# Layer-two norm: squares taken per column half, roots by a third-order step and Newton, other distances at the layer boundary, lambda moved

## The chip, the cores and the metric

One core of one Trainium2 chip runs the whole program. The metric is the device time of one execution in microseconds. The kernel before has three timed runs, 758.97, 760.33 and 760.14, median 760.14; one further execution was taken by the profiler, and its trace is read below. PE is TensorE (matrix products), DVE VectorE, ACT ScalarE, POOL GpSimd, SP the queue that issues transfers.

## The reference

The program is a trunk of two layers over 512 tokens of width 1024, in float32, then a final norm. Cut to what matters here:

```python
def rms_norm(x, g):
    return x * lax.rsqrt(jnp.mean(x * x, axis=-1, keepdims=True) + EPS) * g

# layer 1 (Mamba-2): y is the scan's output, z the gate, 8 groups of 256 columns
u = y * silu(z)
u = u * lax.rsqrt(mean of u*u over each group + EPS) * gate_norm_g
x = x + u @ w_out

# layer 2 (differential attention), 8 heads of width 128, two maps per head
k, v = split(rms_norm(x, kv_norm_g) @ w_kv)
q, gate = split(rms_norm(x, b_norm_g) @ w_in)
lam = exp(sum(lf[0] * lf[1])) - exp(sum(lf[2] * lf[3])) + lambda_init
weights = softmax(scores_1) - lam * softmax(scores_2)
out = rms_norm(weights @ v, sub_g) * (1 - lambda_init)       # per head
x = x + (out * silu(gate)) @ w_out
return rms_norm(x, final_norm_g)
```

Both norms at the head of layer 2 have the same root, so x is normed once, and the two gains go into the weights.

## The kernel before

Tokens are four tiles of 128 (`t`), columns of x two halves of 512 (`n`). Every product is done as three passes, on a high and a low part of each operand (`mm3`: names ending in hi/h and lo/l). A weight arrives by one 1 MB transfer on SP (`raw`), and is split piece by piece: ScalarE writes the high part (`whi`), VectorE the low part (`wlo`), 4 pieces of 512 columns or 8 of 256 (`load`, `lay`).

**Layer 1** runs over items z, g and o and eight groups (`ssd`). At a group's end the scan's parts (`pyd`, `po1`, `po2`) are summed into dx on VectorE and GpSimd, multiplied by the gate, squared on ScalarE into `ss`, the root of four chunks is taken (`rsqrt`), ScalarE applies it (`tmp <- dx, y_y`), and TensorE transposes the result (`pyt`), which ScalarE and VectorE split into yh and yl. A planner that plays through a timeline with costs of its own decides the order of the instructions on each engine here: program order is free as long as `T.on`, `V.on` and `A.on` are False.

**The layer boundary**, called the turn here. Half 0 of the last out-projection is planned with layer 1; half 1 (`last_rows`) runs in an order written by hand: `T.on`, `V.on` and `A.on` are set, so the three engines keep program order. For each tile there are twelve 512-wide products into `po3_1_t`, and then vector work is put off by a distance: `later(n, fn)` emits `fn` when n further units of TensorE work have been emitted (a 512-wide triple counts 2, a 256-wide one 1). Per tile: add (distance 1), square of all 1024 columns (4), root (9), application to the row (root + 5). The same counter paces the weight pieces: `use_b` hands out a segment's weights and queues the next segment's pieces, of which `paced` lays one after every 32/8 = 4 units. Then `turn_rows` transposes the normed row (`btp`), split into b_hi (ScalarE) and b_lo (VectorE); `v_proj(0)` needs of tile t only these rows (`pv`), and `feat_proj("k0k1")` (`pk`) needs all four.

**Layer 2** keeps TensorE in program order; VectorE and ScalarE are planned again. Each head's values are normed by `norm_head` (statistics, `rsqrt`, multiplication of `on`), transposed (`pot`), multiplied by the gate (`og`), split (oh, ol) and projected (`pb`). In the last head three tiles are normed first, and the last tile by itself (`norm_head(7, 3, 4)`). `end(i)` closes the eight half rows: add, square, product with the final gain on GpSimd (`ot`, line 887), and for each tile the last root (`rsqrt1`, names f_) and its application, on ScalarE but for one half on VectorE. `ot` goes out by SP.

Two routines take roots, both from a bit-shift guess and three Newton steps: `rsqrt` for n columns (11 VectorE instructions), and `rsqrt1` for one column (8 instructions, on a value scaled by 2 to the 26).

The program's line 52 is the helper through which instructions are recorded, so rows of the profile are told apart by their tiles; in the changed program the helper is line 53.

Of the kernel before, what the change touches and what calls it, by code (L numbers as in the profile page):

```python
# [60 lines left out]
def trunk(ctx, tc, x, x_t, par, w_dt, w_in, w_out, w_kvqg, w_bo, d_skip, lam_qk, fin_g, out):  # L61
# [58 lines left out]
    def load(i):  # L120

        seg = segs[i]
        src, gains = source(seg)
        nk = 8 if seg[0] in "vkqt" else 4
        w = 2048 // nk
        raw = wp.tile([P, nk, w], F32, tag="raw", name=f"raw{i}", bufs=2)
        fetched[0] += 1

        def split():
            hi = wp.tile([P, nk, w], F32R, tag="whi", name=f"whi{i}", bufs=2)  # L130
            lo = wp.tile([P, nk, w], F32R, tag="wlo", name=f"wlo{i}", bufs=2)
# [15 lines left out]
            return [(head, rest, k, 32 // nk) for k in range(nk)]  # L147

        if i == 0:
            for k in range(nk):  # L150
                load_x(k)
                nc.sync.dma_start(raw[:, k, :], src[:, k * w:(k + 1) * w])
        else:
            nc.sync.dma_start(raw.rearrange("p k n -> p (k n)"), src)
        return split

    def lay(piece):
        head, rest, k, _ = piece
        head(k)
        rest(k)  # L160
# [55 lines left out]
    def rsqrt(v, n, tag, bufs=2):  # L216

        y = small.tile([P, n], F32, tag=f"{tag}_y", name=f"{tag}_y", bufs=bufs)
        c = small.tile([P, n], F32, tag=f"{tag}_c", name=f"{tag}_c", bufs=bufs)
        iy = small.tile([P, n], I32, tag=f"{tag}_i", name=f"{tag}_i", bufs=bufs)  # L220
        V.tensor_scalar(out=iy, in0=v.bitcast(I32), scalar1=1, scalar2=None, op0=ALU.logical_shift_right)
        V.tensor_scalar(out=y.bitcast(I32), in0=iy, scalar1=-1.0, scalar2=float(0x5F3759DF), op0=ALU.mult, op1=ALU.add)
# [4 lines left out]
        return y  # L227

    def rsqrt1(v26, tag, bufs=2):

# [4 lines left out]
        V.tensor_scalar(out=y.bitcast(I32), in0=iy, scalar1=-1.0, scalar2=float(0x5F3759DF - 2 ** 31), op0=ALU.mult, op1=ALU.add)
        for a in (3.0, 12.0, 768.0):
            V.scalar_tensor_tensor(out=c, in0=y, scalar=v26, in1=y, op0=ALU.mult, op1=ALU.mult)
            V.scalar_tensor_tensor(out=y, in0=c, scalar=-a, in1=y, op0=ALU.add, op1=ALU.mult)
        return y
# [249 lines left out]

    decs = {}  # L490
# [21 lines left out]
    def ssd(g):  # L512
# [91 lines left out]
    lq = sm.tile([P, 4, 64], F32, name="lq")  # L604
    nc.sync.dma_start(lq.rearrange("p a d -> p (a d)"), lam_qk.rearrange("a d -> (a d)").partition_broadcast(P))
# [5 lines left out]
    lqv = lq.rearrange("p (a b) d -> p a b d", b=2)  # L611
    lp = lqv[:, :, 0]
    V.tensor_tensor(out=lp, in0=lqv[:, :, 0], in1=lqv[:, :, 1], op=ALU.mult)
    ls = sm.tile([P, 2], F32, name="ls")
    V.reduce_sum(ls, lp, axis=AX.X)
    A.activation(ls, ls, AF.Exp)
    nlam = small.tile([P, 1], F32, name="nlam", bufs=1)
    V.scalar_tensor_tensor(out=nlam, in0=ls[:, 1:2], scalar=-LAM0, in1=ls[:, 0:1], op0=ALU.add, op1=ALU.subtract)

# [39 lines left out]
    T.on = V.on = A.on = True  # L659
    dense[0] = paced(last_rows())  # L660
# [14 lines left out]
    def v_proj(n):  # L675
        wh, wl = use_b(("v", n, 0))
# [113 lines left out]
    def norm_head(h, a=0, b=NT):  # L790
# [88 lines left out]
    def end(i):  # L879
# [12 lines left out]
        V.tensor_scalar(out=v, in0=v, scalar1=2.0 ** 26 / D, scalar2=EPS * 2.0 ** 26, op0=ALU.mult, op1=ALU.add)  # L892
        r = rsqrt1(v, "f")
# [94 lines left out]
```

## Time and profile before

| | us |
|---|---|
| median of three runs | 760.14 (758.97 to 760.33) |
| the profiled execution's own time | 758.57 |
| its span, first to last instruction | 756.8 |
| TensorE busy | 729.8 (96%) |
| VectorE / ScalarE / GpSimd busy | 563.1 / 436.4 / 133.9 |
| TensorE idle, 440 to 468 us of the span (the turn) | 6.2 |
| TensorE idle, 728 to 757 us (the tail) | 14.8 |
| mean granted clock of TensorE | 0.986 |

A row of the timeline reads: start, length, engine, line, operation, output <- inputs, partitions x elements, count, and in brackets the idle time ahead of it with what released it. A row of the waits reads: who waited, for what, total us, times, longest. A row of the time windows: the window, its length, busy time and instructions (x) of PE, PE's weight loads, DVE, ACT and POOL, the granted TensorE clock (1.00 is full), the DMA share and GB/s. Starts of matmuls are exact to the next one's; their lengths overlap.

### The profile page before, as it was taken

How to read it: one execution, taken by the hardware profiler on the slowest of the kernel's cores; microseconds unless marked ns; L12 is line 12 of the kernel's file. 1: busy time of each engine (PE TensorE's matmuls, PEld its weight loads, DVE VectorE, ACT ScalarE, POOL GpSimd, SP SyncE). 2: the span in 40 equal slices, each digit the busy share in tenths (PEclk: the TensorE clock that was granted, in tenths of full speed). 3: DMA queues.
4: the chain of work that ended last, by engine and by line, in shares of the span. 5: the costliest groups of instructions: out<-in, count | busy, mean ns of one | idle time of the engine just before them, and what ended most of it. 6: DMA issues, size and time to landing. Idle time of an engine off the chain costs nothing.

```text
span 756.8 us, 10380 instructions
## 1 busy us (share of the span) xinstructions
PE 729.8 (96%) x3741; PEld 612.2 (81%) x3741; DVE 563.1 (74%) x1286; ACT 436.4 (58%) x943; POOL 133.9 (18%) x162
## 2 busy tenths in 40 slices
PE   9999989999999999999999988999999999999993
PEld 7787867888888888887878867888988888898872
DVE  5589974789769769579977557557767867885987
ACT  6848664564746427548433337567767766656534
POOL 0009251602515024150211110000000000000013
PEclk9999999999999999999999998999999999999997
DMA  9543312132313331213132201331221221132002
GB/s 324 197 159 123 112 61 108 59 116 105 112 55 119 129 136 64 108 61 111 57 112 64 77 27 57 111 112 57 79 90 56 67 101 57 56 112 82 3 0 111
DMA packets 12915, 70.84 MB, mean 94 GB/s; under 512 B 1600, under 2 KB 2112, under 8 KB 5312
## 3 DMA queue, kind: packets, MB, share of 16 engines
q1 hardware_dynamic: 12576, 70.06, 25.7%
q8 instruction: 29, 0.48, 0.3%
q14 instruction: 22, 0.18, 0.1%
q10 hardware_dynamic: 288, 0.12, 0.1%
HBM read 68.02 MB, written 2.16 MB: 93 GB/s over the span
## 4 chain that ended last, share of the span: by engine, by line
PE 75%; DVE 9%; ACT 6%; issue 6%; DMA 2%; POOL 2%; SPq 0%; ACTq 0%; POOLq 0%
PE pg L52 15%; PE po L52 14%; PE pt L52 7%; PE pz L52 6%; PE pq L52 6%; PE pk L52 6%; PE pv L52 6%; PE pb L52 5%; PE pyd L52 3%; PE sc L52 3%; DVE wlo L52 2%; DVE xc L52 2%; ACT whi L52 2%; DVE x_tok L52 1%; PE pyt L52 1%
## 5 line engine op out<-in xcount | busy, mean ns | idle before, releaser
L52 DVE SCALAR_TENSOR_TENSOR wlo<-raw,prm,whi 128x512 fp32r<-128x512 f32 (+1 forms) x256 | 153.4, 643 | 58.6 <-ACT whi L52 58.2
L52 ACT ACTIVATE whi<-raw,prm 128x512 fp32r<-128x512 f32 (+1 forms) x256 | 137.2, 605 | 61.9 <-issue 23.0
L52 PE MATMUL pg<-a_hi,whi 128*128 128x512 f32 x256 | 103.9, 406 | 0.0
L52 PE MATMUL pg<-a_lo,whi 128*128 128x512 f32 x256 | 102.5, 400 | 0.0
L52 PE MATMUL pg<-a_hi,wlo 128*128 128x512 f32 x256 | 102.2, 400 | 0.0
L52 DVE SCALAR_TENSOR_TENSOR xc<-u,prm,xc 128x511 f32<-128x511 f32 (+2 forms) x96 | 80.5, 854 | 7.1 <-ACT xc L52 6.5
L52 PEld LDWEIGHTS pg<-a_hi,whi 128*128 128x128 f32 x256 | 48.2, 188 | 11.0 <-issue 0.2
L52 PEld LDWEIGHTS pg<-a_lo,whi 128*128 128x128 f32 x256 | 48.2, 188 | 10.9 <-issue 0.2
L52 PEld LDWEIGHTS pg<-a_hi,wlo 128*128 128x128 f32 x256 | 48.1, 188 | 10.9
L887 POOL TENSOR_TENSOR ot<-x_tok,fg 128x512 f32<-128x512 f32 x8 | 10.1, 1280 | 262.8 <-DVE o__y L52 259.3
L52 PE MATMUL po<-whi,yh 128*128 128x512 f32 x128 | 51.7, 404 | 0.6 <-ACT yh L52 0.6
L52 PE MATMUL pz<-whi,a_lo 128*128 128x512 f32 x128 | 51.3, 401 | 0.0
L52 PE MATMUL po<-wlo,yh 128*128 128x512 f32 x128 | 50.9, 398 | 0.0
L52 PE MATMUL pz<-wlo,a_hi 128*128 128x512 f32 x128 | 50.8, 397 | 0.0
L52 PE MATMUL po<-whi,yl 128*128 128x512 f32 x128 | 50.6, 399 | 0.0
L52 PE MATMUL pz<-whi,a_hi 128*128 128x512 f32 x128 | 49.9, 401 | 0.0
L52 ACT ACTIVATE xc<-u,prm 128x512 f32<-128x512 f32 x32 | 25.7, 810 | 40.4 <-DVE u L52 40.4
L540 POOL TENSOR_TENSOR xe<-xdt,tok 128x256 f32<-128x256 f32 x24 | 17.7, 765 | 150.2 <-DVE xdt L52 150.2
L52 DVE CUSTOM_DVE_ANT_0 s<-sc,bias 128x128 f32<-128x128 f32 (+3 forms) x64 | 29.8, 487 | 18.1 <-PE sc L52 17.6
L52 ACT ACT_TABLE_LOAD x27 | 34.6, 1283 | 13.6 <-DVE y_c L52 5.2
L502 POOL TENSOR_TENSOR dec<-dec,tok 128x512 f32<-128x512 f32 x32 | 40.2, 1287 | 0.6
L52 PE MATMUL pv<-whi,b_hi 128*128 128x256 f32 x128 | 37.3, 291 | 0.0
(215 smaller groups left out, 1775.1 us busy)
## 6 DMA issues: line engine op xcount, KB each, us to landing
raw<-in_w_in SPq DMA_DIRECT2D x23, 1024.0 KB, 4.8
raw<-in_w_kvqg SPq DMA_DIRECT2D x16, 1024.0 KB, 4.8
dec<-acs_d SPq DMA_DIRECT2D x8, 1024.0 KB, 4.6
raw<-in_w_out SPq DMA_DIRECT2D x8, 1024.0 KB, 4.7
raw<-in_w_bo SPq DMA_DIRECT2D x4, 1024.0 KB, 4.8
xt<-in_x_t SPq DMA_DIRECT2D x8, 256.0 KB, 6.0
x_tok<-in_x SPq DMA_DIRECT2D x4, 512.0 KB, 8.7
out<-ot SPq DMA_DIRECT2D x8, 256.0 KB, 2.1
```

Of the source, the lines that this page charges most:

```text
L52: i = op(*args, **kw)
L502: GP.tensor_tensor(out=dec[:, h], in0=dec[:, h], in1=acs_tok[:, :, R * g + h].unsqueeze(2).to_broadcast([P, NQ, P]), op=ALU.subtract)
L540: GP.tensor_tensor(out=xe[:, c], in0=xdt[:, c], in1=toe_tok[:, c, hs].unsqueeze(2).to_broadcast([P, R, HD]), op=ALU.mult)
L887: GP.tensor_tensor(out=ot[t][:, hs], in0=y, in1=fg[:, hs], op=ALU.mult)
```

## The change

Four edits.

- Squares of the second norm: half 0 of each tile is squared on ScalarE right behind its add in `out_proj(3)`, with sums in `bss[:, 0]`; at the turn only half 1 (128x512) is squared, into `bss[:, 1]`. One VectorE instruction scales `bss[:, 0]` for all four tiles, and each root's first instruction adds the two.
- Roots: one routine; a third-order step and a Newton step take the place of three Newton steps: from 11 to 9 instructions for n columns, from 8 to 7 for one, which the last tile of a head now also uses. The statistics of `norm_head` take two instructions in place of three.
- Distances at the turn: square 4 to 3, root 9 to 6, application root + 5 to root + 4. The pieces of v0's weights are laid every 2 units instead of 4, those of k0k1 after 18 units and then every 2.
- Lambda's load, sums, exponential and `nlam` are emitted behind the turn, not ahead of layer 1's end.

```diff
-    def use_b(seg):
+    def use_b(seg, first=None, pace=None):
...
-            pieces.extend(loaded.pop(i + 1)())
+            new = loaded.pop(i + 1)()
+            pace = pace or 32 // len(new)
+            pieces.extend(p + (pace if k else first or pace,) for k, p in enumerate(new))
...
     def rsqrt(v, n, tag, bufs=2):
...
+        def vyy():
+            if n == 1:
+                V.scalar_tensor_tensor(out=c, in0=y, scalar=v, in1=y, op0=ALU.mult, op1=ALU.mult)
+            else:
+                V.tensor_tensor(out=c, in0=y, in1=v, op=ALU.mult)
+                V.tensor_tensor(out=c, in0=c, in1=y, op=ALU.mult)
...
-        for _ in range(3):
-            V.scalar_tensor_tensor(out=c, in0=y, scalar=-0.5, in1=y, op0=ALU.mult, op1=ALU.mult)
-            V.tensor_tensor(out=c, in0=c, in1=v, op=ALU.mult)
-            V.scalar_tensor_tensor(out=y, in0=c, scalar=1.5, in1=y, op0=ALU.add, op1=ALU.mult)
+        vyy()
+        V.scalar_tensor_tensor(out=c, in0=c, scalar=-10.0 / 3.0, in1=c, op0=ALU.add, op1=ALU.mult)
+        V.scalar_tensor_tensor(out=y, in0=c, scalar=5.0, in1=y, op0=ALU.add, op1=ALU.mult)
+        vyy()
+        V.scalar_tensor_tensor(out=y, in0=c, scalar=-64.0 / 3.0, in1=y, op0=ALU.add, op1=ALU.mult)
         return y
...
                 V.tensor_tensor(out=x_tok[:, t, ns], in0=po, in1=x_tok[:, t, ns], op=ALU.add)
+                if j == 3:
+                    sq = small.tile([P, S], F32, tag="wide", name=f"sq3_{t}", bufs=2)
+                    A.activation(sq, x_tok[:, t, ns], AF.Square, accum_out=bss[:, 0, t:t + 1])
...
-            squares(ss, t, xn[t])
+            A.activation(xn[t][:, 512:D], y, AF.Square, accum_out=bss[:, 1, t:t + 1])
...
-            V.tensor_scalar(out=v, in0=ss[:, t:t + 1], scalar1=2.0 ** 26 / D, scalar2=EPS * 2.0 ** 26, op0=ALU.mult, op1=ALU.add)
-            r = rsqrt1(v, "f")
-            later(5, lambda: A.activation(xn[t], x_tok[:, t], AF.Copy, scale=r))
-
-        later(4, square)
-        later(9, root)
+            V.scalar_tensor_tensor(out=v, in0=bss[:, 1, t:t + 1], scalar=ROOT2 / D, in1=bss[:, 0, t:t + 1], op0=ALU.mult, op1=ALU.add)
+            r = rsqrt(v, 1, "f")
+            later(4, lambda: A.activation(xn[t], x_tok[:, t], AF.Copy, scale=r))
+
+        later(1, lambda: V.tensor_tensor(out=y, in0=po, in1=y, op=ALU.add))
+        later(3, square)
+        later(6, root)
...
-        w = use_b(("o", 3, 1))
+        w = use_b(("o", 3, 1), pace=2)
...
     T.on = V.on = A.on = True
+    later(9, lambda: V.tensor_scalar(out=bss[:, 0], in0=bss[:, 0], scalar1=ROOT2 / D, scalar2=ROOT2 * EPS, op0=ALU.mult, op1=ALU.add))
...
-        wh, wl = use_b(("v", n, 0))
+        wh, wl = use_b(("v", n, 0), *((18, 2) if n == 0 else ()))
...
-        V.scalar_tensor_tensor(out=v, in0=sums[:, 0, a:b], scalar=EPS * P, in1=sums[:, 0, a:b], op0=ALU.mult, op1=ALU.mult)
-        V.tensor_tensor(out=v, in0=v, in1=ss[:, a:b], op=ALU.add)
-        V.tensor_scalar(out=v, in0=v, scalar1=1.0 / P, scalar2=None, op0=ALU.mult)
+        V.scalar_tensor_tensor(out=v, in0=sums[:, 0, a:b], scalar=ROOT2 * EPS, in1=sums[:, 0, a:b], op0=ALU.mult, op1=ALU.mult)
+        V.scalar_tensor_tensor(out=v, in0=ss[:, a:b], scalar=ROOT2 / P, in1=v, op0=ALU.mult, op1=ALU.add)
...
+    lq = cp2.tile([P, 4, 64], F32, tag="gt", name="lq", bufs=3)
+    nc.sync.dma_start(lq.rearrange("p a d -> p (a d)"), lam_qk.rearrange("a d -> (a d)").partition_broadcast(P))
...
+    A.activation(ls, ls, AF.Exp)
+    nlam = small.tile([P, 1], F32, name="nlam", bufs=1)
+    V.scalar_tensor_tensor(out=nlam, in0=ls[:, 1:2], scalar=-LAM0, in1=ls[:, 0:1], op0=ALU.add, op1=ALU.subtract)
     V.on = A.on = False
```

How the order moves, at the turn (two engines), in layer 1 and in the tail.

**The turn, VectorE** (`po_1_t` is tile t's half 1, `wlo` v0's low pieces, `b_v` the root's first instruction). Before, then changed:

```order
L52 TENSOR_TENSOR x_tok<-po_0_3_3699,x_tok 128x512
L52 SCALAR_TENSOR_TENSOR wlo_3725<-raw_3655,prm,whi_3724 128x256 x2
L52 TENSOR_TENSOR x_tok<-po_1_0_3726,x_tok 128x512
L52 SCALAR_TENSOR_TENSOR wlo_3725<-raw_3655,prm,whi_3724 128x256 x2
L52 TENSOR_SCALAR b_v_3767<-bss 128x1
```

```order
L53 TENSOR_TENSOR x_tok<-po_0_3_3686,x_tok 128x512
L53 SCALAR_TENSOR_TENSOR wlo_3707<-raw_3636,prm,whi_3706 128x256 x4
L53 TENSOR_SCALAR bss<-bss 128x4
L53 TENSOR_TENSOR x_tok<-po_1_0_3708,x_tok 128x512
L53 SCALAR_TENSOR_TENSOR wlo_3707<-raw_3636,prm,whi_3706 128x256 x2
L53 SCALAR_TENSOR_TENSOR b_v_3747<-bss 128x1
```

Four low pieces instead of two stand ahead of tile 0's add.

**The turn, ScalarE** (`xn<-x_tok,f_y` is the application, `bss<-x_tok` a square; the first `xn` number is tile 0, the second tile 1). Before, then changed:

```order
L52 ACTIVATE whi_3724<-raw_3655,prm 128x256 x2
L52 ACTIVATE xn_3751,bss<-x_tok 128x1024
L52 ACTIVATE whi_3724<-raw_3655,prm 128x256 x2
L52 ACTIVATE xn_3784,bss<-x_tok 128x1024
L52 ACTIVATE whi_3724<-raw_3655,prm 128x256
L52 ACTIVATE xn_3751<-x_tok,f_y 128x1024
```

```order
L53 ACTIVATE sq_0_3652,bss<-x_tok 128x512
L53 ACTIVATE sq_1_3668,bss<-x_tok 128x512
L53 ACTIVATE sq_2_3684,bss<-x_tok 128x512
L53 ACTIVATE sq_3_3700,bss<-x_tok 128x512
L53 ACTIVATE whi_3706<-raw_3636,prm 128x256 x5
L53 ACTIVATE xn_3740,bss<-x_tok 128x512
L53 ACTIVATE whi_3706<-raw_3636,prm 128x256 x3
L53 ACTIVATE xn_3740<-x_tok,f_y 128x1024
L53 ACTIVATE xn_3775,bss<-x_tok 128x512
```

Tile 1's square stood ahead of tile 0's application, and now stands behind it; half 0's squares are new ahead of all.

**Group 0's root chain in layer 1, ScalarE** (`dx` is the gated output, `tmp,ss<-dx` its square, `tmp<-dx,y_y` the application, `dec` the decays). Before, then changed:

```order
L52 ACT_TABLE_LOAD
L52 ACTIVATE xc_915<-xc_915 128x512
L52 ACTIVATE tmp_711,ss_710<-dx_676 128x256 x2
L52 ACT_TABLE_LOAD
L52 ACTIVATE dec_1010<-dec_1010 128x1024
L52 ACTIVATE whi_929<-raw_927,prm 128x512 x4
L52 ACTIVATE dec_1010<-dec_1010 128x1024
L52 ACT_TABLE_LOAD
L52 ACTIVATE zs_0_1179<-pz_0_923,ar_col 128x512
L52 ACTIVATE tmp_711<-dx_676,y_y 128x256 x4
```

```order
L53 ACTIVATE tmp_708,ss_707<-dx_673 128x256 x3
L53 ACTIVATE dec_1005<-dec_1005 128x1024 x2
L53 ACT_TABLE_LOAD
L53 ACTIVATE xc_910<-xc_910 128x512
L53 ACTIVATE whi_924<-raw_922,prm 128x512 x4
L53 ACTIVATE tmp_708<-dx_673,y_y 128x256 x4
```

Between the last squares and the application stood two table loads and a zs; now one table load and an xc stand there.

**The tail, VectorE** (`o__` are the last head's single root, `on` the normed values, `pb_t_n` the half rows). Before, then changed:

```order
L52 TENSOR_TENSOR x_tok<-pb_0_0_6747,x_tok 128x512
L52 SCALAR_TENSOR_TENSOR o__y<-o__c,o__y 128x1
L52 TENSOR_TENSOR x_tok<-pb_0_1_6751,x_tok 128x512
L52 SCALAR_TENSOR_TENSOR o__c<-o__y 128x1
L52 TENSOR_TENSOR o__c<-o__c,o_v_3_6766 128x1
L52 SCALAR_TENSOR_TENSOR o__y<-o__c,o__y 128x1
L52 TENSOR_TENSOR x_tok<-pb_1_0_6755,x_tok 128x512
L52 TENSOR_TENSOR on_6422<-on_6422,o__y 128x128
```

```order
L53 SCALAR_TENSOR_TENSOR o__c<-o__y,o_v_3_6729 128x1
L53 SCALAR_TENSOR_TENSOR o__y<-o__c,o__y 128x1
L53 TENSOR_TENSOR x_tok<-pb_0_0_6710,x_tok 128x512
L53 TENSOR_TENSOR on_6391<-on_6391,o__y 128x128
L53 TENSOR_TENSOR x_tok<-pb_0_1_6714,x_tok 128x512
L53 TENSOR_TENSOR x_tok<-pb_1_0_6718,x_tok 128x512
```

`on` moves from behind the third add to behind the first. TensorE's own order is unchanged from out-projection 3 to the end.

More of the change, by code (lines that the diff above doesn't have):

```diff
@@ L31 @@
 BIG = 1e30
+ROOT2 = (1024.0 / 27.0) ** 2
 ORDER_B = "v0 k0k1 q0t0 q1t1 k2k3 q2t2 v1 q3t3 k4k5 q4t4 v2 q5t5 k6k7 q6t6 b0 v3 q7t7 b1 b2 b3".split()
@@ L145, in rest @@
                     V.tensor_tensor(out=lo[:, k, :], in0=raw[:, k, :], in1=hi[:, k, :].bitcast(F32), op=ALU.subtract)
-            return [(head, rest, k, 32 // nk) for k in range(nk)]
+            return [(head, rest, k) for k in range(nk)]
         if i == 0:
@@ L157, in lay @@
     def lay(piece):
-        head, rest, k, _ = piece
+        head, rest, k = piece[:3]
         head(k)
@@ L265, in scales @@
     def scales(tag, ss):
-        V.tensor_scalar(out=ss, in0=ss, scalar1=1.0 / D, scalar2=EPS, op0=ALU.mult, op1=ALU.add)
+        V.tensor_scalar(out=ss, in0=ss, scalar1=ROOT2 / D, scalar2=ROOT2 * EPS, op0=ALU.mult, op1=ALU.add)
         col = res.tile([P, NT], F32, tag="r_col", name=f"{tag}r_col")
@@ L488, in stream_a @@
             yield
+    bss = small.tile([P, 2, NT], F32, name="bss", bufs=1)
     decs = {}
@@ L588, in ssd @@
         v4 = small.tile([P, NQ], F32, tag="v4", name=f"v4{g}")
-        V.tensor_scalar(out=v4, in0=ss4, scalar1=1.0 / 256.0, scalar2=EPS, op0=ALU.mult, op1=ALU.add)
+        V.tensor_scalar(out=v4, in0=ss4, scalar1=ROOT2 / 256.0, scalar2=ROOT2 * EPS, op0=ALU.mult, op1=ALU.add)
         r4 = rsqrt(v4, NQ, "y")
@@ L603, in trunk @@
     decays(0)
-    lq = sm.tile([P, 4, 64], F32, name="lq")
-    nc.sync.dma_start(lq.rearrange("p a d -> p (a d)"), lam_qk.rearrange("a d -> (a d)").partition_broadcast(P))
     dense[0] = stream_a()
@@ L610, in trunk, with row_norm @@
     until("o3")
[L611 to L618, printed above, removed]
     hh, hl = new_h("b")
     done.clear()
-    ss = small.tile([P, NT], F32, tag="bss", name="bss", bufs=1)
     xn = {}
-    def row_norm(t):
+    def row_norm(t, po):
+        y = x_tok[:, t, 512:D]
         def square():
             xn[t] = small.tile([P, D], F32, tag="wide", name=f"xn{t}", bufs=2)
-            squares(ss, t, xn[t])
+            A.activation(xn[t][:, 512:D], y, AF.Square, accum_out=bss[:, 1, t:t + 1])
         def root():
             v = small.tile([P, 1], F32, tag="f_v", name=f"b_v{t}", bufs=2)
-            V.tensor_scalar(out=v, in0=ss[:, t:t + 1], scalar1=2.0 ** 26 / D, scalar2=EPS * 2.0 ** 26, op0=ALU.mult, op1=ALU.add)
-            r = rsqrt1(v, "f")
-            later(5, lambda: A.activation(xn[t], x_tok[:, t], AF.Copy, scale=r))
-        later(4, square)
-        later(9, root)
+            V.scalar_tensor_tensor(out=v, in0=bss[:, 1, t:t + 1], scalar=ROOT2 / D, in1=bss[:, 0, t:t + 1], op0=ALU.mult, op1=ALU.add)
[4 more added lines that the diff above has]
+        later(6, root)
     def last_rows():
-        w = use_b(("o", 3, 1))
+        w = use_b(("o", 3, 1), pace=2)
         for t in range(NT):
@@ L646, in last_rows @@
                 yield 2
-            y = x_tok[:, t, 512:D]
-            later(1, lambda po=po, y=y: V.tensor_tensor(out=y, in0=po, in1=y, op=ALU.add))
-            row_norm(t)
+            row_norm(t, po)
     due = [0.0]
@@ L891, in end @@
         V.tensor_tensor(out=v, in0=ss[:, t, 0:1], in1=ss[:, t, 1:2], op=ALU.add)
-        V.tensor_scalar(out=v, in0=v, scalar1=2.0 ** 26 / D, scalar2=EPS * 2.0 ** 26, op0=ALU.mult, op1=ALU.add)
-        r = rsqrt1(v, "f")
+        V.tensor_scalar(out=v, in0=v, scalar1=ROOT2 / D, scalar2=ROOT2 * EPS, op0=ALU.mult, op1=ALU.add)
+        r = rsqrt(v, 1, "f")
         for n in range(2):
```

15 lines of the change are left out of this document (5 added, 10 removed).

## The prediction

> **What bounds the kernel now.** I read the page's busy times first, then the page of waits on TensorE, then the time windows.
>
> ```profile
> PE 729.8 (96%) x3741; PEld 612.2 (81%) x3741; DVE 563.1 (74%) x1286; ACT 436.4 (58%) x943; POOL 133.9 (18%) x162
> PE btp L52 <- ACT xn L52: 6.1, 3, 2.7
> PE pyt L52 <- ACT tmp L52: 2.8, 1, 2.8
> PE pot L52 <- DVE f_v L52: 2.4, 1, 2.4
> 115.00:328.00 213.00, 213.00 (x1063) 178.19 (x1062) 163.41 (x274) 114.01 (x198) 62.04 (x73) 0.99 0.27 96
> 440.00:468.00 28.00, 21.82 (x109) 18.09 (x108) 18.65 (x61) 16.57 (x31) 0.55 (x1) 0.90 0.11 38
> 728.00:757.00 29.00, 14.22 (x60) 10.92 (x58) 21.54 (x79) 12.21 (x29) 10.07 (x8) 0.81 0.19 73
> ```
>
> TensorE bounds it: 729.8 of 756.8 us, and its matmul count stays 3741. From 115 to 328 it is never idle, so a shorter vector chain there buys nothing. A gain must come out of the few places where TensorE waits: the turn (btp, 6.1 us), group 0's transposes (pyt, 2.8) and the tail (pot, 2.4, and what follows TensorE's last matmul). In the windows the seventh column is the granted clock; it falls at just these places:
>
> ```profile
> 452.25:455.66 3.41, 2.88 (x11) 2.69 (x12) 2.22 (x11) 2.05 (x4) 0.00 (x0) 0.50 0.00 0
> 459.10:462.50 3.40, 3.40 (x32) 3.37 (x29) 3.14 (x14) 1.77 (x5) 0.00 (x0) 1.00 0.46 123
> 465.90:469.30 3.40, 3.40 (x18) 3.40 (x17) 3.12 (x13) 3.10 (x6) 0.00 (x0) 0.50 0.00 0
> 738.97:742.40 3.43, 3.43 (x9) 2.64 (x8) 2.99 (x7) 1.08 (x4) 2.02 (x2) 0.50 0.00 0
> 114.30:117.70 3.40, 3.36 (x14) 2.77 (x14) 1.16 (x2) 3.12 (x7) 0.00 (x0) 0.50 0.51 214
> 452.78 1.97 PE L52 MATMUL btp<-ident,xn 128*128 128x128 f32 x8 [2.71 <-ACT xn L52]
> 458.77 1.10 PE L52 MATMUL btp<-ident,xn 128*128 128x128 f32 x8 [0.75 <-ACT xn L52]
> 465.30 1.44 PE L52 MATMUL btp<-ident,xn 128*128 128x128 f32 x8 [2.64 <-ACT xn L52]
> ```
>
> Behind each idle of 2.4 to 2.8 us lie 3.4 us at half clock, behind the 0.75 us idle none. Half of 3.4 us of matmul work is lost where TensorE has work throughout, about 1.5 us as I count it. So the turn costs 6.1 + 2 x 1.5 = 9.1 us, group 0 costs 4.3, the tail 3.9 at TensorE.
>
> **The turn: why xn came late.**
>
> ```profile
> 444.51 0.69 DVE L52 TENSOR_TENSOR x_tok<-po,x_tok 128x512 f32<-128x512 f32 x1 [0.57 <-PE po L52]
> 447.63 0.15 DVE L52 TENSOR_SCALAR b_v<-bss 128x1 f32<-128x1 f32 x1
> 449.42 0.69 DVE L52 TENSOR_TENSOR x_tok<-po,x_tok 128x512 f32<-128x512 f32 x1
> 450.14 1.06 ACT L52 ACTIVATE xn<-x_tok 128x1024 f32<-128x1024 f32 x1 [2.95 <-DVE x_tok L52]
> 451.59 1.13 ACT L52 ACTIVATE xn<-x_tok,f_y 128x1024 f32<-128x1024 f32 x1
> 734.85 0.60 ACT L52 ACTIVATE pb<-x_tok 128x512 f32<-128x512 f32 x1 [1.90 <-DVE x_tok L52]
> 441.36 0.91 ACT L52 ACTIVATE whi<-raw,prm 128x256 fp32r<-128x256 f32 x2 [5.47 <-PE po L52]
> 451.72 0.48 DVE L52 SCALAR_TENSOR_TENSOR wlo<-raw,prm,whi 128x256 fp32r<-128x256 f32 x1 [1.61 <-ACT whi L52]
> 440.66 2.48 DVE L52 TENSOR_TENSOR x_tok<-po,x_tok 128x512 f32<-128x512 f32 x4 [3.93 <-PE po L52]
> 477.10 0.39 PE L52 MATMUL pk<-b_hi,whi 128*128 128x512 f32 x1
> 477.33 0.40 PE L52 MATMUL pk<-b_lo,whi 128*128 128x512 f32 x1
> ```
>
> Root 0 runs from 447.63 to about 449.5 (nine instructions, then the add of 449.42), but ACT applies it at 451.59 only: the square of tile 1 stands ahead of it in ACT's order, that waits for tile 1's add, and that stands behind root 0. The change orders apply 0 ahead of square 1. I replay it with these rows' durations; a 512-wide matmul starts 0.233 us after the one before it (477.10, 477.33), so twelve take 2.8 us, and so do a value block's 24 of half the width. Eight transposes take 0.9 (the 1.10 of 458.77 less the overlap with what follows).
>
> Half 0's four squares (0.69 apart, from the 128x512 row of 0.60 plus part of its accumulator read) follow the adds of 440.66 and end at 444.2. Five hi pieces at 0.41 end at 446.2, and four lo pieces that follow them now stand ahead of the first add: it comes at 446.35, 1.84 later than before. That is the price of the new pace, and it eats most of what the halved square saves. Then add 0.69, half square 0.6, two lo pieces, root of eight instructions 1.7, apply 1.13: xn0 at 451.5 instead of 452.7, so btp0 idles 1.5 us instead of 2.7. Tile 1: add at 451.0, square, root to 454.2, apply to 455.4; TensorE gets there at 451.5 + 0.9 + 2.8 = 455.2, idle 0.2. Tile 2: four lo pieces run among its root's instructions, apply ends 460.0; TensorE arrives 455.4 + 0.9 + 2.8 = 459.1, idle 0.9. Tile 3 is ready in time. After btp2 TensorE has three value blocks and btp3 left before pk, besides its own: 460.1 + 2 x 0.9 + 3 x 2.8 = 470.3, against 477.10. **Gain 6.8** without a slow window. An idle of 1.5 us lies between 0.75 (none) and 2.43 (one), so it may still draw one: 5.3 with it. I take **5.8**, nearer to the one with it; the bounds are 8.3 (no idle at btp0) and 1.3 (only xn0's 1.2 us survives and both slow windows stay).
>
> The Trainium skill's page "TensorE: Matmul & The Clock Gate", section "What's actually happening", has free-running windows of about 3.4 us and half clock after at least one idle window. The 3.4 us agree with the rows; that one whole idle window is needed does not, since 2.71 us idle was enough here. By that rule no slow window could follow 1.5 us, and the turn would give 6.8.
>
> **Roots and squares elsewhere** (layer 1, heads 0 to 6): two instructions fewer per root of four, about 0.4 us, hidden by a busy TensorE (115:328). But the planner sorts layer 1 anew from the new costs. In TensorE's work, counted in matmuls, the stretch from a group's last pyd to its pyt shrinks by 1.2 us in group 0, 3.7 in group 5, 4.4 in group 6, 0.9 to 1.6 in groups 1 to 4.
>
> ```profile
> 111.16 0.75 DVE L52 SCALAR_TENSOR_TENSOR wlo<-raw,prm,whi 128x512 fp32r<-128x512 f32 x1
> 111.72 1.28 ACT L52 ACT_TABLE_LOAD   x1
> 113.61 1.69 ACT L52 ACTIVATE tmp<-dx,y_y 128x256 f32<-128x256 f32 x4
> 114.16 2.15 PE L52 MATMUL pyt<-ident,tmp 128*128 128x128 f32 x8 [2.76 <-ACT tmp L52]
> 342.85 1.69 ACT L52 ACTIVATE tmp<-dx,y_y 128x256 f32<-128x256 f32 x4
> 343.85 1.18 PE L52 MATMUL pyt<-ident,tmp 128*128 128x128 f32 x8
> ```
>
> The root in group 0 ends just ahead of the lo piece of 111.16. Then a table load and a zs stood between it and tmp. In the change they don't, the root runs in one piece, and one table load fewer lies in the chain: tmp could start between 110.3 (nothing else late) and 113.0 (the decay exponential waits for POOL's mask as before). Less the 1.2 us by which TensorE asks earlier, group 0 gains between 3.7 (slow window gone) and loses 0.6. In group 5 tmp's first quarter was done 0.6 us before pyt; the root loses its four interleaved lo pieces, about 3.8 us, against 3.7 that TensorE asks earlier: nothing, or at worst 3.1 + 1.5 lost. I take **1.5** gained in layer 1, with ends 3.7 and -5.2.
>
> **The tail.**
>
> ```profile
> 735.43 0.83 DVE L52 SCALAR_TENSOR_TENSOR o__c<-o__y 128x1 f32<-128x1 f32 x1
> 736.29 1.18 DVE L52 TENSOR_TENSOR o__c<-o__c,o_v 128x1 f32<-128x1 f32 x1
> 738.19 0.28 DVE L52 TENSOR_TENSOR on<-on,o__y 128x128 f32<-128x128 f32 x1
> 738.62 0.30 PE L52 MATMUL pot<-ident,on 128*128 128x128 f32 x1 [2.43 <-DVE f_v L52]
> 734.95 2.51 POOL L887 TENSOR_TENSOR ot<-x_tok,fg 128x512 f32<-128x512 f32 x2 [259.34 <-DVE o__y L52]
> 743.44 4.99 POOL L887 TENSOR_TENSOR ot<-x_tok,fg 128x512 f32<-128x512 f32 x4 [1.30 <-DVE f_v L52]
> 747.27 1.18 DVE L52 SCALAR_TENSOR_TENSOR f_y<-f_c,f_y 128x1 f32<-128x1 f32 x1
> 752.41 0.72 ACT L52 ACTIVATE ot<-ot,f_y 128x512 f32<-128x512 f32 x1 [0.40 <-DVE f_y L52]
> ```
>
> The last head's single root had 14 instructions to `on`, nine remain, and its last now stands ahead of the second add: `on` is due at 735.0 instead of 738.47, before TensorE is free at 736.2. Wait and slow window go: TensorE's end comes 3.9 earlier. The end of the kernel does not: the two instructions of 0.83 and 1.18 us do what the turn's root does in 0.2 each, and the second ends with POOL's pair of products (737.46). POOL has eight products at 1.25, 10.0 us in all, which from 734.95 end at 745.0 at best, against 748.43. Adding the 4.7 us from there to the last ot (753.13) gives 749.7, 3.4 earlier. The roots now stand more of their time under POOL, so I take **2** of it; bounds 0 and 4.
>
> The Trainium skill's "GPSIMD Engine Reference", section "1. Specifications", has GpSimd's SBUF interface shared with VectorE's instructions with two SBUF inputs; the two stretched rows agree. By that rule the gain ends where POOL does, at 3.4 us.
>
> **Lambda** moves behind the turn: two DVE instructions, one more table load there (1.28 in the row above) and an exponential, all while TensorE works through pk from 470.3 on. Its load follows a 1 MB weight load on SP's queue and precedes the next; VectorE's bias and eight lo pieces queue behind it, whose weights TensorE takes 11 us after pk's start as before. I cost it at **0**; it shows from about 8 us late. At the start it frees about 1 us of VectorE that bounded nothing.
>
> **Sum:** 758.57 (the profiled run, span 756.8) - 5.8 - 1.5 - 2 = 749.3. The profiled run lies 1.57 under the median of 760.14, so the forecast is **751**.
>
> **Rivals.**
> - *The turn's wait only shifts.* The lo pieces ahead of add 0 come later than replayed, btp0 idles over 2 us again and btp2 too, both slow windows stay. For it: the add already loses 1.84. Against it: apply 0 no longer waits for square 1. Turn 1.3, rest 3.5: 755.
> - *All goes well:* turn 8.3, group 0 3.7, tail 4: 744. Against it: POOL's 10.0 us, and the 1.84 at the first add.
> - *The plan does not carry the change:* layer 1 loses its 5.2, the tail gives 0, the turn 5: 760, no change.
> - *Slower: late lo pieces in layer 1.* Where the roots now run in one piece, the four lo pieces of the next weights come behind them; in group 5 behind three convolution taps and two more products too, about 3 us later. TensorE would then wait at pg or pz. It decides from 9.3 us, 1.2 us in each of eight groups; at 3 us in five groups it is 15 - 9.3 = 6 lost: 766. Against it: the page of waits shows no wait of pg or pz, and most weights are first used at the same place in TensorE's work as before.
>
> **Chances.** Forecast 0.56; shifted wait 0.17; all well 0.11; no change 0.08; slower 0.08. Two tenths of a per cent, 1.5 us, is what a measurement of this kernel tells from none. Faster 0.84, same 0.08, slower 0.08. The range 744.5 to 759.5 takes in the first two and about half of the third and fourth, and leaves out some 0.17.
>
> **What would show it.** Right: the wait btp <- xn falls from 6.1 to about 2.6, pk starts some 7 us earlier relative to the last layer-1 matmul, no 0.50 window at btp2; pot waits for nothing; POOL's products run on end in the tail and the last ot is about 2 us earlier. Wrong: btp0 waits over 2 us; new rows pg or pz <- wlo, or pyt <- tmp in groups 5 and 6; a wait of VectorE on lq after the turn.

## The result, and the profile after

The changed kernel takes 747.8 us (median of four runs, 747.46 to 749.01) against 760.09 before: ratio 0.9844, 95% interval 0.9827 to 0.9861, 12.3 us faster. Measured again beside other kernels it took 748.34 against 758.99, ratio 0.9863 (0.9842 to 0.9885). The profiled execution has a span of 745.7 us against 756.8. The page's busy times and its waits on TensorE (who waited, for what: total us, times, longest):

```profile
PE 723.1 (97%) x3741; PEld 606.7 (81%) x3741; DVE 553.5 (74%) x1232; ACT 437.9 (59%) x951; POOL 132.3 (18%) x162
PE pxt L53 <- ACT xc L53: 2.8, 2, 2.6
PE btp L53 <- ACT xn L53: 2.0, 2, 1.3
PE pcb L53 <- ACT xc L53: 2.0, 1, 2.0
```

The waits of pyt and pot are gone and that of btp falls from 6.1 to 2.0 us. Two waits in layer 1 have grown, pxt and pcb; before they were:

```profile
PE pxt L52 <- ACT xc L52: 1.2, 2, 0.7
PE pcb L52 <- ACT xc L52: 0.2, 1, 0.2
```

In the windows (seventh column: the granted clock) the turn now runs at full clock; the tail's 0.81 now lies behind TensorE's last matmul, which starts at 731.85 us.

```profile
437.00:462.00 25.00, 22.91 (x130) 18.89 (x129) 18.19 (x59) 17.49 (x39) 0.56 (x1) 1.00 0.14 48
718.00:746.00 28.00, 14.00 (x69) 11.05 (x67) 19.71 (x70) 12.67 (x31) 10.02 (x8) 0.81 0.20 75
```

Cut at four events, each run's span shows where time went: the first add of half 0 ahead of the turn, the first pk, the start of the last head's last value products, and the end of the last ot. The rest is what is then left of the span, which the page gives to 0.1 us. The second column is the part of layer 1 that follows the start of the 37th product into pz, layer 1's first projection, where the start of the program is over. The last column lists the half-clock windows (3.41 us at a granted clock of 0.50) that fell while TensorE had work, by their starts. The tail is told below with the rest: 23.25 + 3.67 = 26.92 us before, 20.36 + 4.02 = 24.38 in the changed kernel.

| profiled run | layer 1 | of it, from the 37th pz | turn | layer 2 | tail to last ot | rest | span | half clock from |
|---|---|---|---|---|---|---|---|---|
| before | 440.66 | 426.06 | 36.44 | 252.78 | 23.25 | 3.67 | 756.8 | 114.3, 452.3, 465.9, 739.0 |
| changed | 439.86 | 425.46 | 29.35 | 252.11 | 20.36 | 4.02 | 745.7 | none |
| changed, second (after2) | 441.52 | 426.08 | 29.36 | 252.13 | 20.37 | 4.02 | 747.4 | 72.4 |
| b_lam | 436.50 | 421.90 | 36.40 | 252.04 | 22.73 | 3.63 | 751.3 | 448.2, 461.8, 734.9 |
| b_dist | 442.28 | 426.88 | 32.20 | 252.78 | 22.71 | 3.63 | 753.6 | 117.1, 458.4 |
| u_dist | 441.21 | 425.86 | 32.81 | 252.13 | 20.38 | 3.97 | 750.5 | 72.2, 454.5 |
| u_pace | 441.51 | 426.38 | 30.18 | 252.12 | 20.36 | 4.03 | 748.2 | 71.7 |
| u_sq | 441.66 | 426.18 | 29.85 | 252.11 | 20.37 | 4.01 | 748.0 | 72.4 |
| u_lam | 439.86 | 425.03 | 29.30 | 252.76 | 20.42 | 3.96 | 746.3 | 350.0 |
| u_o1 | 439.53 | 425.33 | 29.35 | 252.12 | 22.37 | 3.93 | 747.3 | none |
| u_roots | 437.54 | 421.87 | 30.33 | 252.01 | 22.89 | 3.63 | 746.4 | none |
| x_both2 | 440.10 | 425.84 | 30.63 | 252.11 | 20.22 | 3.24 | 746.3 | 455.4 |
| x_l1 | 437.38 | 421.96 | 29.37 | 252.11 | 20.37 | 4.77 | 744.0 | none |
| x_best | 436.43 | 421.74 | 29.37 | 252.11 | 20.23 | 3.16 | 741.3 | none |

Of the 11.1 us between the first two rows 7.1 come from the turn, 2.5 from the tail (with the rest), 0.8 from layer 1 and 0.7 from layer 2. Layer 1's first column can't be compared to better than a microsecond: the 37th product into pz starts anywhere from 14.20 us (u_o1) to 15.67 us (u_roots), and between the changed kernel's two profiles, which run the same program, it moves from 14.40 to 15.44. The second column is free of that. The turn's rows of the changed kernel (timeline, VectorE, ScalarE, TensorE):

```profile
445.29 0.69 DVE L53 TENSOR_TENSOR x_tok<-po,x_tok 128x512 f32<-128x512 f32 x1
447.63 0.15 DVE L53 SCALAR_TENSOR_TENSOR b_v<-bss 128x1 f32<-128x1 f32 x1
...
449.34 1.15 ACT L53 ACTIVATE xn<-x_tok,f_y 128x1024 f32<-128x1024 f32 x1 [1.35 <-DVE f_y L53]
450.67 0.63 ACT L53 ACTIVATE xn<-x_tok 128x512 f32<-128x512 f32 x1 [0.18 <-DVE x_tok L53]
...
450.54 1.09 PE L53 MATMUL btp<-ident,xn 128*128 128x128 f32 x8 [1.27 <-ACT xn L53]
454.36 1.09 PE L53 MATMUL btp<-ident,xn 128*128 128x128 f32 x8
458.98 1.09 PE L53 MATMUL btp<-ident,xn 128*128 128x128 f32 x8 [0.73 <-ACT xn L53]
469.21 0.39 PE L53 MATMUL pk<-b_hi,whi 128*128 128x512 f32 x1
```

The first add comes 1.6 us later than before, counted from half 0's adds (445.29 - 439.86 = 5.43 against 3.85), as the pieces ahead of it cost. Still the application follows the root at once, and tile 1's square stands behind it.

### The profile page after: what moved, and what is told of

It reads as the page before. It is cut to its first block, busy times and chain, and to the rows that moved or that the text cites. A ratio compares the mean times of both kernels' runs of the same rounds, so it can differ in the third digit from the quotient of the medians.

```text
span 745.7 us, 10346 instructions
## 1 busy us (share of the span) xinstructions
PE 723.1 (97%) x3741; PEld 606.7 (81%) x3741; DVE 553.5 (74%) x1232; ACT 437.9 (59%) x951; POOL 132.3 (18%) x162
## 4 chain that ended last, share of the span: by engine, by line
PE 81%; DVE 6%; ACT 5%; issue 4%; DMA 2%; POOL 0%; SPq 0%; ACTq 0%; POOLq 0%; DVEq 0%
PE pg L53 16%; PE po L53 14%; PE pz L53 9%; PE pt L53 7%; PE pq L53 6%; PE pk L53 6%; PE pv L53 6%; PE pb L53 5%; PE pyd L53 4%; PE sc L53 3%; DVE wlo L53 2%; ACT whi L53 1%; DVE xc L53 1%; DMA raw<-in_w_in 1%; PE psA L53 1%
## 5 line engine op out<-in xcount | busy, mean ns | idle before, releaser
L53 DVE SCALAR_TENSOR_TENSOR wlo<-raw,prm,whi 128x512 fp32r<-128x512 f32 (+1 forms) x256 | 155.6, 652 | 47.1 <-ACT whi L53 46.5
L53 ACT ACTIVATE tmp<-dx 128x256 f32<-128x256 f32 x32 | 13.2, 412 | 45.1 <-DVE dx L53 45.1
```

The lines of the kernel that those rows point to most:

```text
L53: i = op(*args, **kw)
```

## The experiments

A name that begins with u_ is the changed kernel with one part undone, b_ is the kernel before with one part done, x_ goes beyond the change. Ratios are against the kernel before on the same chip, with 95% intervals.

**b_dist: the distances alone.**

```diff
-            later(5, lambda: A.activation(xn[t], x_tok[:, t], AF.Copy, scale=r))
+            later(4, lambda: A.activation(xn[t], x_tok[:, t], AF.Copy, scale=r))
-        later(4, square)
-        later(9, root)
+        later(3, square)
+        later(6, root)
```

> The kernel before with the new distances alone (square 3, root 6, application root + 4, add still 1), full squares, old roots, old pace of the pieces. Theory 1 (the order is what counts: application 0 no longer behind square 1): replayed with the durations of before, xn0 is ready at 450.4 instead of 452.7, btp0 to btp2 wait 0.4, 0.9 and 1.1 us, no slow window, and pk comes 6 to 7 us earlier; time 753 to 754.5. Theory 2 (the halved squares, the shorter roots and the pace carry the turn): 1 to 3 us, time 757 to 759.

754.69 us, 0.9939 (0.9923 to 0.9955). The turn falls by 4.2 us, with one half-clock window left:

```profile
452.02 1.09 PE L52 MATMUL btp<-ident,xn 128*128 128x128 f32 x8 [0.32 <-ACT xn L52]
457.95 1.60 PE L52 MATMUL btp<-ident,xn 128*128 128x128 f32 x8 [2.04 <-ACT xn L52]
...
455.95 0.91 ACT L52 ACTIVATE whi<-raw,prm 128x256 fp32r<-128x256 f32 x2 [1.20 <-PE po L52]
456.76 1.14 ACT L52 ACTIVATE xn<-x_tok,f_y 128x1024 f32<-128x1024 f32 x1
```

Theory 1's order, at two thirds of its size: btp0 hardly waits, as replayed (0.4), but btp1 waits 2.04 instead of 0.9. ScalarE's rows show why: two high pieces stand ahead of tile 1's application, and they wait for TensorE's last out-projection products, whose weights lie in the buffer that they overwrite. TensorE, done with those products, then waits for the application behind them. In the changed kernel no such piece stands there; nor does one in u_pace below, which has the old pace, so it is not the pace that keeps them behind. By a count in the code these are k0k1's last pieces, emitted behind the turn, where the planner is free again to choose their place; that this is how they got ahead is argued, not tried.

**u_dist: all but the distances** (the three lines above, the other way round).

> The changed kernel with the old distances (square 4, root 9, application root + 5) and all else as changed. Theory 1: application 0 stands behind square 1 again, btp0 comes at 452.6 instead of 450.5 with 3 us idle and a slow window: 2 to 3.6 us slower than the changed kernel, 750 to 751.5. Theory 2: within 0.5 us of the changed kernel, 748.

752.95 us, 0.9924 (0.9908 to 0.9941). btp0 waits longer than in the kernel before:

```profile
453.91 1.48 PE L53 MATMUL btp<-ident,xn 128*128 128x128 f32 x8 [3.30 <-ACT xn L53]
```

The turn is 3.5 us longer than in the changed kernel, as theory 1 said. The time lies above its 750 to 751.5; in the profile layer 1 is 1.4 us longer too, 0.9 of it in the start and the rest with a half-clock window. So the distances are worth 3.5 to 4.2 of the turn's 7.1 us, alone or last.

**u_pace, u_sq: the pieces' old pace; the full squares (with the root's first instruction on one sum again).**

```diff
-        w = use_b(("o", 3, 1), pace=2)
+        w = use_b(("o", 3, 1))
-        wh, wl = use_b(("v", n, 0), *((18, 2) if n == 0 else ()))
+        wh, wl = use_b(("v", n, 0))
```

> The changed kernel with the weight pieces at the old pace of 4 at the turn. Two low pieces instead of four stand ahead of the first add. Theory 1: the first add comes 1 us earlier (444.3), btp0 too, so it waits 0.3 us instead of 1.3; the later tiles bound pk then, so the gain is 0 to 1 us: 747 to 748. Theory 2 (the faster pace is needed for the value products): pv waits for low pieces, 1 us or more slower, above 749.

```diff
-                if j == 3:
-                    sq = small.tile([P, S], F32, tag="wide", name=f"sq3_{t}", bufs=2)
-                    A.activation(sq, x_tok[:, t, ns], AF.Square, accum_out=bss[:, 0, t:t + 1])
...
-            A.activation(xn[t][:, 512:D], y, AF.Square, accum_out=bss[:, 1, t:t + 1])
+            A.activation(xn[t], x_tok[:, t], AF.Square, accum_out=bss[:, 1, t:t + 1])
```

> The changed kernel with the squares of all 1024 columns at the turn again (no squares of half 0 ahead of it). Theory 1 (order decides, and half 0's squares keep the high pieces and so the first add waiting for 2.5 us on ScalarE): the first add comes over 1 us earlier, each square takes 0.4 longer, so the turn from half 0's adds to pk is 29.2 to 29.9 us against 29.35 of the changed kernel; time 747.5 to 748.5. Theory 2 (the halved squares carry the rest of the turn's gain that the distances alone don't give, 2.9 us): turn above 31.5, time 750 or more.

u_pace: 749.39 us, 0.9874 (0.9856 to 0.9891); u_sq: 749.63, 0.9866 (0.9851 to 0.9881). First three rows of u_pace, then one of u_sq:

```profile
454.50 1.15 ACT L53 ACTIVATE xn<-x_tok,f_y 128x1024 f32<-128x1024 f32 x1 [0.80 <-DVE f_y L53]
455.56 0.89 ACT L53 ACTIVATE whi<-raw,prm 128x256 fp32r<-128x256 f32 x2
...
459.99 0.39 PE L53 MATMUL pv<-wlo,b_hi 128*128 128x256 f32 x1 [0.62 <-DVE wlo L53]
```

```profile
461.02 1.09 PE L53 MATMUL btp<-ident,xn 128*128 128x128 f32 x8 [1.64 <-ACT xn L53]
```

With the old pace btp0 waits 0.5 us instead of 1.3, as theory 1 said, but the value products wait 0.6 for low pieces, as theory 2 said, and btp1 and btp3 wait 0.4 each where they waited for nothing: the turn is 0.8 us longer, so the new pace pays on the whole. The two high pieces of b_dist stand behind tile 1's application here (455.56 against 454.50). With full squares btp2 waits 1.6 instead of 0.7: the turn is 0.5 us longer (29.85, inside theory 1's 29.2 to 29.9). Both times lie above theory 1's; in the profiles layer 1 is 1.7 and 1.8 us longer than in the changed kernel, 0.7 and 1.1 of it in the start, the rest with a half-clock window.

**u_lam, b_lam: lambda at its old place in the changed kernel; lambda's move alone in the kernel before.** u_lam's edit (b_lam's is its reverse):

```diff
+    lq = sm.tile([P, 4, 64], F32, name="lq")
+    nc.sync.dma_start(lq.rearrange("p a d -> p (a d)"), lam_qk.rearrange("a d -> (a d)").partition_broadcast(P))
     dense[0] = stream_a()
...
     until("o3")
+    lqv = lq.rearrange("p (a b) d -> p a b d", b=2)
...
+    V.scalar_tensor_tensor(out=nlam, in0=ls[:, 1:2], scalar=-LAM0, in1=ls[:, 0:1], op0=ALU.add, op1=ALU.subtract)
```

> The changed kernel with lambda's load and five instructions at their old place. Theory 1 (the move is worth nothing where it goes, and layer 1's new waits pxt and pcb come from the roots' new costs): both waits stay, within 1.5 us of the changed kernel, 747 to 749. Theory 2 (the new wait of pxt, 2.6 us at 70 us, comes from lambda's absence in the plan of the first groups): it falls to 0.7, time 745 to 746.5.

> The kernel before with lambda's load and five instructions moved behind the turn, and nothing else. Theory 1 (the move makes the planner lay layer 1 out anew, as in u_roots, whose TensorE order it shares): half 0's adds at the turn start at 437.5 instead of 440.7 us, the wait pyt of 2.8 us goes; layer 2 from pk to the last value product takes 252.1 instead of 252.8 as in every run with lambda moved; turn and tail stay as before (36.4 and 26.9, less if a slow window is missed): 3 to 4 us faster than before, 755 to 756.5. Theory 2 (the move alone is worth nothing, as predicted, and the better layer 1 needs the halved squares): 758 to 760.

u_lam: 748.53 us, 0.9852 (0.9837 to 0.9867). b_lam: 752.81 us, 0.9918 (0.9899 to 0.9937): the move alone is worth 6 us by the ratio, more than theory 1's 3 to 4. Waits and group 0's rows of b_lam:

```profile
PE btp L52 <- ACT xn L52: 6.0, 3, 2.7
PE pot L52 <- DVE f_v L52: 2.5, 1, 2.5
PE pxt L52 <- ACT xc L52: 1.1, 3, 0.5
108.61 1.69 ACT L52 ACTIVATE tmp<-dx,y_y 128x256 f32<-128x256 f32 x4
109.23 1.56 PE L52 MATMUL pyt<-ident,tmp 128*128 128x128 f32 x8
```

The waits at the turn and in the tail stay, and the two take 36.40 and 26.4 us against 36.44 and 26.9; but layer 1 is 4.2 us shorter, because the planner lays group 0 out anew, so that tmp is ready in time, and the half-clock window behind pyt goes too. Whether the load, the five instructions or their tiles' places turn the plan was not tried apart. Layer 2 takes 0.7 us less (below). Taken back out of the changed kernel the move makes no such difference (u_lam), since the other edits without it also make the planner lay group 0 out anew: pyt has no wait there either. u_lam's waits:

```profile
PE pcb L53 <- ACT xc L53: 2.0, 1, 2.0
PE pxt L53 <- ACT xc L53: 0.8, 2, 0.4
```

So pcb's 2.0 us come with the new roots, and pxt's 2.6 only with both edits. Neither theory had both.

**u_o1, u_roots: the last head's single root in its old form; all roots and statistics in their old form** (the diff of `rsqrt` and `norm_head` above, the other way round; in u_o1 only where `b - a == 1`).

> The changed kernel, with only the last head's single root in its old form (three statistics instructions, three Newton steps, 14 instead of 9 instructions). Theory 1 (the tail's gain of 2.9 us comes from this root): pot waits 2 us or more again with a slow window, 2 to 3 us slower, 750 to 751. Theory 2 (the tail's end is set by POOL's eight products and TensorE's end does not matter): 0 to 0.7 slower, 748 to 748.5.

> The changed kernel with the old roots and the old statistics of the heads everywhere. Theory 1 (roots matter in the tail and, through the plan, in layer 1's second half): pot waits over 2 us again, tail 1.9 to 2.9 us longer; the wait of pcb (2.0 us at 349 us) goes with the old plan of the later groups; turn 0.2 to 0.5 longer; time 748 to 750.5. Theory 2 (each root's two instructions count on the path): 13 roots of 0.4 us on top, 753 or more.

u_o1: 749.19 us, 0.9879 (0.9862 to 0.9897). u_roots: 747.87 us, 0.9842 (0.9828 to 0.9857). The wait of u_o1, and three of u_roots:

```profile
PE pot L53 <- DVE f_v L53: 2.7, 1, 2.7
```

```profile
PE pot L53 <- DVE f_v L53: 2.5, 1, 2.5
PE pxt L53 <- ACT xc L53: 1.1, 3, 0.5
PE pcb L53 <- ACT xc L53: 0.2, 1, 0.2
```

The old single root makes the tail 1.9 us longer (26.30 against 24.38); no half-clock window follows its wait, and the time stays below theory 1's 750. With all roots old the tail loses 2.1 and the turn 1.0, but layer 1 gains 2.3, and 3.6 from the 37th pz on: pxt and pcb wait about as little as before. The two nearly cancel, and the time is that of the changed kernel, below theory 1's 748 to 750.5. The roots, then, pay in the tail and at the turn, and cost in layer 1.

**x_l1, x_best, after2: the old root in layer 1 alone; with it, fewer products on GpSimd; the changed kernel beside them.**

```diff
-        r4 = rsqrt(v4, NQ, "y")
+        r4 = rsqrt_old(v4, NQ, "y")
```

The root in `scales`, of layer 1's first norm, changes the same way. x_best adds to this:

```diff
-        GP.tensor_tensor(out=ot[t][:, hs], in0=y, in1=fg[:, hs], op=ALU.mult)
+        if t < 2:
+            GP.tensor_tensor(out=ot[t][:, hs], in0=y, in1=fg[:, hs], op=ALU.mult)
...
+            if t >= 2:
+                V.scalar_tensor_tensor(out=o, in0=x_tok[:, t, hs], scalar=r, in1=fg[:, hs], op0=ALU.mult, op1=ALU.mult)
```

> The changed kernel with the old root (three Newton steps, eleven instructions) in layer 1's norms alone; turn, heads and tail keep the new ones. Theory 1 (the roots' new costs make the planner lay layer 1 out with the waits pxt 2.6 and pcb 2.0; longer roots give the better plan): half 0's adds at the turn start at 437.5 us instead of 439.9, turn and tail as in the changed kernel; span 743.4, time 745 to 746. Theory 2 (shorter roots are better for layer 1 and u_roots had luck in its waits): 748 or more.

> The kernel x_l1 and, for the last two tiles, VectorE's multiplication by root and gain in one instruction, so that GpSimd makes four products instead of eight. By the 0.9 us that this gave behind TensorE's last matmul in x_both2: 744 to 745.5. If VectorE's extra 1.3 us cost more than the stretch that goes: no better than x_l1.

> The changed kernel again, beside the two above on one chip: 747 to 749 by its first measurement, with the waits pxt 2.6 and pcb 2.0; a slow window behind either costs 1.5 us, depending on where the 3.4 us windows fall.

Side by side: x_l1 746.03 us, 0.9829 (0.9805 to 0.9852); x_best 743.37, 0.9799 (0.9775 to 0.9822); the changed kernel 748.34. x_l1 shows theory 1's layer 1 (437.38; from the 37th pz on 3.5 us less than in the changed kernel), and the time lies just above its 746: the rest is 4.77 us instead of 4.02, since ot's last transfer landed 3.3 us after its issue instead of 2.6. x_best came out below its 744 to 745.5, 5 us faster than the changed kernel by these medians. In the profiles of the two it is 6.1 us: 1.0 behind TensorE's last matmul and 5.1 in layer 1, of which the start takes 0.7, the new plan 3.7 and the half-clock window that the changed kernel met there the rest.

**x_both2: a later first piece at the turn, and x_best's tail, on the changed kernel.**

```diff
-        w = use_b(("o", 3, 1), pace=2)
+        w = use_b(("o", 3, 1), first=10, pace=2)
```

> The changed kernel with two edits: v0's first weight piece at the turn waits for 10 units, so that tile 0's add stands ahead of all pieces; and for the last two tiles VectorE multiplies by root and gain in one instruction from x, so that GpSimd makes four products instead of eight. Theory 1: btp0 no longer waits (1.3 us saved), VectorE's small instructions are no longer stretched behind GpSimd's last four products (2.6 us of stretch less, 1.3 us of new products more): 745.5 to 747. Theory 2 (the next tiles bound pk anyway, and VectorE is the tail's bound): 747.5 to 749.

749.46 us, 0.9871 (0.9855 to 0.9888): neither theory. btp0 no longer waits, but two pieces of k0k1's weights now stand ahead of tile 1's application and wait for the buffer, as in b_dist, so that btp1 waits 2.04 us, with a half-clock window:

```profile
453.23 0.91 ACT L53 ACTIVATE whi<-raw,prm 128x256 fp32r<-128x256 f32 x2 [0.91 <-PE po L53]
454.05 1.13 ACT L53 ACTIVATE xn<-x_tok,f_y 128x1024 f32<-128x1024 f32 x1
...
455.23 1.82 PE L53 MATMUL btp<-ident,xn 128*128 128x128 f32 x8 [2.04 <-ACT xn L53]
```

The turn is 1.3 us longer, the tail 0.9 us shorter (23.46 against 24.38).

## Why the prediction was right, and where it was not

747.8 lies in the range of 744.5 to 759.5, 3.2 us below the forecast of 751; the sum in profiled executions was 749.3 against 747.46. The turn and the tail came out by the mechanisms that were forecast. That the sum came out so near is partly luck, because two steps on layer 1 were wrong in opposite ways: taken in the order before, b_lam, x_l1, changed kernel, layer 1 takes 426.1, 421.9, 422.0 and 425.5 us from the 37th pz on, so that lambda's move gave 4.2 us where 0 was forecast, and the new roots of layer 1 cost 3.5 where the new plan was to gain 1.5. The shares depend on the order: without lambda's move all the other edits give 1.0 there (u_lam, 425.0).

- **Turn, 5.8 forecast, 7.1 measured.** The mechanism was the one named: the waits at btp0 to btp2 are 1.27, 0 and 0.73 against 1.5, 0.2 and 0.9, and the replay gave 6.8. Mis-sized was only the half-clock window: 1.0 of its 1.5 us was allowed for an idle of 1.5 us, and none came. The delay of 1.84 us at the first add was there (1.6). Not seen was that high pieces that wait for a weight buffer can get ahead of tile 1's application, as in b_dist and x_both2, where btp1 waits 2.04 us each time.
- **Layer 1, 1.5 forecast, 0.8 measured (0.6 from the 37th pz on), and 0.9 lost in the second profile.** pyt's wait went, and tmp started at 110.62, inside 110.3 to 113.0. What failed is "nothing, or at worst" elsewhere: the bounds looked at the stretch from pyd to pyt alone. The plan also moved the convolution's taps, and TensorE waits for xc at pxt and pcb instead:

```profile
70.94 0.66 PE L53 MATMUL pxt<-ident,xc 128*128 128x128 f32 x4 [2.63 <-ACT xc L53]
351.03 1.16 PE L53 MATMUL pcb<-xc,xc 128*128 128x128 f32 x8 [1.96 <-ACT xc L53]
```

  The rival with pg or pz waiting for late low pieces did not occur: TensorE waits for the convolution instead.
- **Lambda, forecast 0.** This was the step most wrong, and hidden in the sum: alone the move is worth 6 us (b_lam), beside the other edits only some 0.7, in layer 2 (u_lam). The argument looked at where the instructions go, where it holds (nlam is written at 469.40 behind a wait of 1.69 us that TensorE does not feel), and at the start asked only what the freed time bounds, not what the planner does with it.
- **Tail, 2 forecast, 2.5 measured.** pot no longer waits, TensorE ends 3.85 us earlier (3.9 forecast), and the end follows by less, since GpSimd's products set it. TensorE's last transpose and matmul, those products, an instruction of VectorE's beside them with one input and one with two, and the last ot:

```profile
727.34 0.27 PE L53 MATMUL pot<-ident,on 128*128 128x128 f32 x1
731.85 0.39 PE L53 MATMUL pb<-whi,ol 128*128 128x512 f32 x1
...
726.32 5.09 POOL L891 TENSOR_TENSOR ot<-x_tok,fg 128x512 f32<-128x512 f32 x4 [258.26 <-DVE x_tok L53]
732.30 4.93 POOL L891 TENSOR_TENSOR ot<-x_tok,fg 128x512 f32<-128x512 f32 x4 [0.89 <-DVE f_c L53]
734.11 0.14 DVE L53 TENSOR_SCALAR f_y<-f_i 128x1 int32<-128x1 int32 x1
736.02 1.23 DVE L53 TENSOR_TENSOR f_v<-fss 128x1 f32<-128x1 f32 x1
739.73 1.95 ACT L53 ACTIVATE ot<-ot,f_y 128x512 f32<-128x512 f32 x3 [0.35 <-DVE f_y L53]
```

  From GpSimd's end (737.23) to the last ot (741.68) it is 4.45 us, against 4.7 in the working. That the end comes 0.9 us earlier in x_both2, which takes four of the products away, agrees, though that edit changes VectorE's and ScalarE's last multiplications too. Of VectorE's 128x1 instructions there only those with two inputs are stretched (the f_v of 736.02 takes 1.23 us); those with one take 0.13 to 0.15 us beside the same products.
- **Layer 2, forecast 0, measured 0.7:** not foreseen; see below.

## What to carry to other kernels

Where a planner sets the order, an edit's price is not that of its instructions: five small ones moved from the start were worth 6 us, and shorter roots cost 3.5 us in layer 1, through orders far from either; so build each edit alone, and compare the page of waits and not only the sum. Where order is written by hand, ask first what stands ahead of the critical instruction on its engine: distances that put one application ahead of a square gave 3.5 to 4.2 us, halving the square 0.5. Put stages side by side before reading a total, and count the first one from a product behind the start, since a half-clock window falls into one profile of a program and not into another, and the start itself moves by a microsecond.

## What the runs showed of the hardware

**Half-clock windows lie on a fixed grid.** In every profile the starts of half-clock windows lie whole multiples of 3.413 us apart (before: 114.33, 452.25, 465.90, 738.97), and the grid's place differs from one execution to the next. What they go by, in these rows, is how much of one grid window TensorE idles. In the fourteen profiles every window that held 1.96 us or more of one wait was followed by one at half clock (15 of 15); of the 26 that held 1.0 to 1.76 us one was (1.51 us, in b_dist, ahead of pyt's transposes). A wait of 2.63 us that lies across a border, as pxt's in the changed kernel (some 1.3 us on either side), costs nothing more; in the second profile the same wait, 2.18 us, lay inside one window, and the half-clock window behind it cost another 1.2: the same products start 0.6 us later than in the first profile ahead of it (71.52 against 70.94) and 1.8 later behind it (75.80 against 74.01). First that second profile, then the changed kernel's first (its grid has a border at 69.6):

```profile
68.94:72.35 3.41, 1.23 (x8) 0.79 (x7) 3.38 (x3) 1.91 (x2) 3.41 (x3) 1.00 0.76 308
72.35:75.76 3.41, 3.41 (x11) 2.62 (x10) 3.38 (x7) 2.23 (x3) 2.73 (x4) 0.50 0.00 0
```

```profile
69.55:72.96 3.41, 2.02 (x11) 1.76 (x12) 3.34 (x4) 1.37 (x3) 3.41 (x4) 1.00 0.59 250
72.96:76.37 3.41, 3.25 (x17) 2.42 (x16) 3.41 (x7) 3.38 (x4) 1.53 (x3) 1.00 0.00 0
```

The start differs as well: TensorE's 24 `warm` products take 5.38 us in the second profile and 4.41 in the first, and the first four into pz 1.63 and 1.20. With the window this accounts for the 1.7 us by which layer 1 differs between these executions of one program. The Trainium skill's "TensorE: Matmul & The Clock Gate", section "What's actually happening", states the free-running window of 3413 ns, which these rows bear out, and half clock after at least one idle window; here 57% of a window was enough.

**The last projection's matmuls run 2% faster where lambda is moved.** In all eleven runs with lambda moved layer 2 takes 252.0 to 252.1 us, in the three with lambda at its old place 252.8. Of the difference 0.5 us lies in pb; before, then changed (ns: least, median, most):

```profile
L52 PE MATMUL pb<-wlo,oh x64: 389/396/628, 655.9 to 744.0; 128*128 128x512 f32 x64
```

```profile
L53 PE MATMUL pb<-wlo,oh x64: 387/389/398, 647.9 to 731.6; 128*128 128x512 f32 x64
```

TensorE's order there is the same. The edit takes lambda's two tiles out of layer 1's pool and puts them into others, so other tiles may lie at other places in memory; that this is the cause was not tried and stays open.
